# A product of token and row halves that needs no sum of weights moved from sixth to second place in each seven-product step

## The chip, the cores and the metric

The kernel runs on one core of a Trainium2 chip. The metric is the device time of one execution in microseconds (us); lower is better. The core's engines are TensorE (PE: matrix products; its loading of weights is listed as PEld), VectorE (DVE), ScalarE (ACT), GpSimd (POOL) and SyncE (SP), which here only starts transfers from HBM. Each engine works through its own queue in order, and engines wait for one another through semaphores.

## What is computed

One block of a decoder over 512 tokens with 1024 features, in float32. The change concerns the two feed-forward halves (`ffn1_*`, `ffn2_*`) alone; between them stand a gating mixer and a differential attention, which are not touched.

```python
def swiglu(h, w_gate, w_up, w_down):
    return (jax.nn.silu(h @ w_gate) * (h @ w_up)) @ w_down

x = x + 0.5 * swiglu(rms_norm(x, ffn1_norm), ffn1_w_gate, ffn1_w_up, ffn1_w_down)
...                                        # the mixer, another residual
x = x + 0.5 * swiglu(rms_norm(x, ffn2_norm), ffn2_w_gate, ffn2_w_up, ffn2_w_down)
```

`w_gate` and `w_up` are 1024 x 2816, `w_down` is 2816 x 1024.

## The kernel before

Data lies with features on the 128 partitions and tokens along the row, so x is 8 tiles of 128 x 512. To keep float32 accuracy each operand is split into a high and a low part: ScalarE casts the high part (line 139), VectorE subtracts it from the source (line 140), and a product is three matmuls, high x high, high x low and low x high. For weights the parts are `w_hi` and `w_lo`.

The 2816 inner features are taken 256 at a time, in 11 pieces numbered q. The first two of each half are computed plainly (`plain_quad`). The other nine go through `quad`, lines 304 to 363, and are called steps here: 18 in the kernel. A step regards its work as a product of 2 x 2 blocks: the tokens are cut into two halves of 256, the 1024 rows of the weights into two halves of 512, and the columns into gate and up. Instead of eight block products it makes seven, of sums of blocks. The block of weights b11 is gate of the first rows, b21 gate of the second rows, b12 and b22 the same for up. A11 and A12 are the first tokens with the first and the second rows, A22 the second tokens with the second rows; S0 to S3 are sums of such blocks, prepared once in each half by `half_sums`. A product, `product`, line 314, is named here after its operand. It splits its weights and makes 24 matmuls of 128 x 256 (all on line 324). In the order of the code a step is:

- A11 with b11 into bank a; ScalarE copies a as p1 (line 331)
- S1 with t3 = b12 + b22 into bank c; copied as p7
- S2 with t2 = t3 + b11, added into a; copied as u2
- A22 with t2 + b21, added into c; VectorE adds c and u2: the gate of the second tokens (line 346)
- S0 with b11 + b12, added into a; VectorE adds a into p7 (line 350)
- A12 with b21 into bank e; VectorE adds e and p1: the gate of the first tokens (line 352)
- the gate is multiplied by the norm's factors `r_bc` (line 357) and put through Silu on ScalarE (line 358)
- S3 with b22, added into a; VectorE multiplies a and p7 into the two halves of the gate (lines 360, 361), and the result is split as a_hi and a_lo

The sums of weights are made by VectorE (`total`, line 311). So bank a is written by A11, S2, S0 and S3 in turn, and read between them.

After four, four and three pieces the down projection adds their share, 8 products with matmuls of 128 x 512 (lines 125 to 127). This end of a group needs a_hi and a_lo of the last step from its nineteenth matmul on, its thirteenth in the third group.

Buffers set how far the splits run ahead. There are four pairs of w_hi and w_lo, used in turn, so the weights of a product go into the pair of four products before. There are six buffers for raw weights, used in turn too, four of them by a step (its loads are in the order b11, b12, b22, b21, by SyncE, line 307), and two for the sums.

The queue of each engine is laid out when the kernel is built: a scheduler goes by the order of the code and by its own estimates of how long operations take, and may put an instruction ahead of one that stands earlier in the code and would still have to wait. So the built order, and not the code alone, tells what stands behind what.

Of the kernel before, what the change touches and what calls it, by code (L numbers as in the profile page):

```python
# [17 lines left out]
ALU = mybir.AluOpType  # L18
# [28 lines left out]
HT = T // 2  # L47
# [11 lines left out]
def decoder_block(  # L59
# [25 lines left out]
    nc = tc.nc  # L85
# [10 lines left out]
    def bank(pool=acc):  # L96
        return pool.tile([P, T], F32, name="bank_" + pool.name, tag=pool.name)
# [3 lines left out]
    def any_bank():  # L101
        turn_of[0] ^= 1
        return bank(acc if turn_of[0] else att)

    def scratch():
        return tmp.tile([P, T], F32, name="scratch", tag="scratch")
# [31 lines left out]
    def split(hi, lo, src):  # L138
        latest["hi"] = nc.scalar.copy(hi, src)  # L139
        latest["lo"] = nc.vector.tensor_tensor(lo, src, hi, op=ALU.subtract)  # L140
# [104 lines left out]
    def ffn(pool, gu, dn, norm, xt, finish, load, prepare, again, plain):  # L245
# [4 lines left out]
        def parts():  # L250
            own = turns["w"] % 4 == 3
            turns["w"] += 1
            src = pool if own else wp
            return tuple(src.tile([P, 1024], F32R, name=f"w_{n}", tag=f"w_{n}") for n in ("hi", "lo"))

        def raw_tile():
            own = turns["raw"] % 6 > 1
            turns["raw"] += 1
            if own:
                return pool.tile([P, 1024], F32, name="w_raw", tag="w_raw", bufs=4)  # L260
            return wp.tile([P, 1024], F32, name="w_raw", tag="w_raw", bufs=RAWS)

        def activated(q):
            hi, lo = (pool.tile([P, 2, T], F32R, name=f"a_{n}{q}", tag=f"a_{n}{q % 4}") for n in ("hi", "lo"))
            a_hi[q], a_lo[q] = hi, lo
            return hi, lo

        def block(q, i):

            h = i // 2  # L270
            return gu[2 * q : 2 * q + 2, (i + h) % 2, :, h * T : (h + 1) * T].rearrange("f p c -> p f c")
# [30 lines left out]
            split(*activated(q), g)  # L302

        def quad(q):
            b11, b12, b22, b21 = (raw_tile() for _ in range(4))
            for i, t in enumerate((b11, b12, b22, b21)):
                nc.sync.dma_start(out=t.rearrange("p (f c) -> p f c", f=2), in_=block(q, i))

            def total(x, y):
                t = pool.tile([P, 1024], F32, name="w_sum", tag="w_sum", bufs=2)  # L310
                nc.vector.tensor_tensor(t, x, y, op=ALU.add)
                return t

            def product(ps, w, x, first=False):
                hi, lo = parts()
                split(hi, lo, w)
                of = operand(x)
                for f in range(2):
                    o = ps[:, f * HT : (f + 1) * HT]
                    for kt in range(HK):  # L320
                        s = slice((f * HK + kt) * P, (f * HK + kt + 1) * P)
                        x_hi, x_lo = of(kt)
                        for i, (l, r) in enumerate(((hi, x_hi), (hi, x_lo), (lo, x_hi))):
                            nc.tensor.matmul(  # L324
                                o, lhsT=l[:, s], rhs=r, start=first and f == kt == i == 0,
                                stop=kt == HK - 1 and i == 2, skip_group_check=True,
                            )

            def kept(ps):
                t = scratch()  # L330
                nc.scalar.copy(t, ps)
                return t

            two = dict(f=2)
            g = pool.tile([P, 2, T], F32, name="g", tag="g", bufs=2)
            a, c, e = bank(acc), bank(att), any_bank()
            product(a, b11, "A11", True)
            p1 = kept(a)
            t3 = total(b12, b22)
            product(c, t3, "S1", True)  # L340
            p7 = kept(c)
            t2 = total(t3, b11)
            product(a, t2, "S2")
            u2 = kept(a)
            product(c, total(t2, b21), "A22")
            nc.vector.tensor_tensor(
                g[:, :, HT:], c.rearrange("p (f t) -> p f t", **two), u2.rearrange("p (f t) -> p f t", **two), op=ALU.add
            )
            product(a, total(b11, b12), "S0")
            nc.vector.tensor_tensor(p7, a, p7, op=ALU.add)  # L350
            product(e, b21, "A12", True)
            nc.vector.tensor_tensor(
                g[:, :, :HT], e.rearrange("p (f t) -> p f t", **two), p1.rearrange("p (f t) -> p f t", **two), op=ALU.add
            )
            if q in prepare:
                prepare[q]()
            nc.vector.tensor_tensor(g, g, r_bc.unsqueeze(1).to_broadcast([P, 2, T]), op=ALU.mult)
            nc.scalar.activation(g, g, AF.Silu)
            product(a, b22, "S3")
            nc.vector.tensor_tensor(g[:, :, :HT], a.rearrange("p (f t) -> p f t", **two), g[:, :, :HT], op=ALU.mult)  # L360
            nc.vector.tensor_tensor(g[:, :, HT:], p7.rearrange("p (f t) -> p f t", **two), g[:, :, HT:], op=ALU.mult)
            split(*activated(q), g)

        y = []
        for f0 in range(0, NF, 8):
            n = min(8, NF - f0)
            for q in range(f0 // 2, (f0 + n) // 2):
                if q < plain:
                    plain_quad(q)
                else:  # L370
                    quad(q)
                if q == plain - 1:
                    for kt in range(HK):
                        add_sums(kt, xt[kt], xt[kt + HK])
            for j in range(KD):
# [21 lines left out]
                else:  # L397
                    for ts, ps in zip(cols, banks):
                        t = scratch()[:, ts]
# [646 lines left out]
```

## Time and profile before

| | us |
|---|---|
| median of 3 runs | 1154.8 |
| lowest, highest | 1154.61, 1155.35 |
| the profiled execution | 1154.97 |
| its span, first to last instruction | 1153.3 |
| TensorE busy | 1145.2 (99%) |
| VectorE busy | 845.9 (73%) |
| ScalarE busy | 590.7 (51%) |
| GpSimd busy | 28.6 (2%) |

The span is 1.7 us shorter than the execution, and TensorE is idle for some 8 us of it. Ends of matmuls are modelled and overlap, so in the rows below the distance from one matmul's start to the next says more than a matmul's length. The mean granted clock of TensorE is 1.000 over the span. A bracket at a row's end is the idle time of the engine just before and what ended it.

### The profile page before, as it was taken

Reading aid. Unit: us, or ns where it says so; the run is one execution under the profiler, and the core shown is the slowest. Engines: PE = TensorE matmul, PEld = TensorE weight load, DVE = VectorE, ACT = ScalarE, POOL = GpSimd, SP = SyncE. Lnnn points to the kernel's source line nnn. Section 1 sums busy time; section 2 is a strip of 40 time slices with the busy share of each in tenths; the row PEclk is TensorE's granted clock in tenths of the full one; section 3 lists DMA queues with packets and bytes.
Section 4 is the critical chain, followed back from the end, with each engine's and each line's share of the span. In section 5 each row is a group of like instructions: output and inputs, shape, how many; then the busy total and the mean of one; then the engine's idle time right before and its main releaser. Section 6 shows DMA issues by size and latency. Waiting matters only on the chain.

```text
span 1153.3 us, 16684 instructions
## 1 busy us (share of the span) xinstructions
PE 1145.2 (99%) x6568; PEld 996.8 (86%) x6568; DVE 845.9 (73%) x1374; ACT 590.7 (51%) x856; POOL 28.6 (2%) x57
## 2 busy tenths in 40 slices
PE   8999999999999999999999999999999999999998
PEld 7898899989987888888878887888899899988997
DVE  6985489768876767867878976655887369877874
ACT  6653356414544554667587966334545235523440
POOL 0000000000002000000000000000000000000000
PEclk9999999999999999999999999999999999999999
DMA  8144132623324323222212124334424223541222
GB/s 276 53 132 143 55 116 75 227 64 110 90 94 147 118 74 92 74 92 74 74 55 73 56 79 160 92 123 163 152 74 147 73 74 110 166 148 67 87 82 73
DMA packets 46861, 122.08 MB, mean 106 GB/s; under 512 B 4560, under 2 KB 5856, under 8 KB 46784
## 3 DMA queue, kind: packets, MB, share of 16 engines
q1 hardware_dynamic: 44208, 113.26, 30.7%
q0 software_dynamic: 2432, 7.75, 2.0%
q8 instruction: 51, 0.84, 0.3%
q14 instruction: 26, 0.21, 0.1%
q10 hardware_dynamic: 144, 0.01, 0.0%
HBM read 114.72 MB, written 6.29 MB: 105 GB/s over the span
## 4 chain that ended last, share of the span: by engine, by line
PE 95%; ACT 2%; DMA 1%; DVE 1%; issue 0%; SPq 0%; ACTq 0%; DVEq 0%
PE bank_acc L324 20%; PE bank_att L324 11%; PE bank_acc L127 11%; PE bank_acc L125 11%; PE bank_acc L126 11%; PE bank_att L127 5%; PE bank_att L126 5%; PE bank_att L125 5%; PE bank_acc L537 4%; PE bank_acc L539 4%; PE bank_acc L538 4%; DMA w_raw<-in_gu 1%; PE bank_att L667 1%; PE bank_att L668 1%; PE bank_att L695 1%
## 5 line engine op out<-in xcount | busy, mean ns | idle before, releaser
L139 ACT CAST w_hi<-w_raw 128x1024 fp32r<-128x1024 f32 (+2 forms) x192 | 191.8, 1004 | 281.2 <-PE bank_acc L126 91.8
L140 DVE TENSOR_TENSOR w_lo<-w_raw,w_hi 128x1024 fp32r<-128x1024 f32 (+2 forms) x192 | 224.0, 1170 | 78.2 <-ACT w_hi L139 73.3
L139 ACT CAST w_hi<-w_sum 128x1024 fp32r<-128x1024 f32 x72 | 75.5, 1050 | 138.7 <-PE bank_acc L324 62.0
L324 PE MATMUL bank_acc<-s_lo,w_hi 128*128 128x256 f32 x432 | 121.6, 281 | 0.0
L324 PE MATMUL bank_acc<-s_hi,w_hi 128*128 128x256 f32 x432 | 121.5, 281 | 0.0
L324 PE MATMUL bank_acc<-s_hi,w_lo 128*128 128x256 f32 x432 | 121.4, 281 | 0.0
L140 DVE TENSOR_TENSOR w_lo<-w_sum,w_hi 128x1024 fp32r<-128x1024 f32 x72 | 87.6, 1220 | 26.0 <-ACT w_hi L139 26.0
L125 PE MATMUL bank_acc<-xg_hi,w_hi 128*128 128x512 f32 x224 | 89.3, 399 | 1.3 <-ACT w_hi L139 1.3
L127 PE MATMUL bank_acc<-xg_hi,w_lo 128*128 128x512 f32 x224 | 89.2, 398 | 1.0 <-DVE w_lo L140 1.0
L537 PE MATMUL bank_acc<-w_hi,xg_hi 128*128 128x512 f32 x224 | 88.9, 397 | 0.0
L126 PE MATMUL bank_acc<-xg_lo,w_hi 128*128 128x512 f32 x224 | 88.8, 396 | 0.0
L538 PE MATMUL bank_acc<-w_lo,xg_hi 128*128 128x512 f32 x224 | 88.6, 395 | 0.0
L539 PE MATMUL bank_acc<-w_hi,xg_lo 128*128 128x512 f32 x224 | 88.5, 395 | 0.0
L324 PEld LDWEIGHTS bank_acc<-s_hi,w_hi 128*128 128x128 f32 x432 | 81.6, 189 | 0.0
L324 PEld LDWEIGHTS bank_acc<-s_hi,w_lo 128*128 128x128 f32 x432 | 81.7, 189 | 0.0
L324 PEld LDWEIGHTS bank_acc<-s_lo,w_hi 128*128 128x128 f32 x432 | 81.6, 189 | 0.0
L125 PE MATMUL bank_acc<-a_hi,w_hi 128*128 128x512 f32 (+1 forms) x182 | 71.1, 391 | 0.0
L126 PE MATMUL bank_acc<-a_lo,w_hi 128*128 128x512 f32 (+1 forms) x182 | 71.1, 391 | 0.0
L127 PE MATMUL bank_acc<-a_hi,w_lo 128*128 128x512 f32 (+1 forms) x182 | 71.1, 391 | 0.0
L126 PE MATMUL bank_att<-a_lo,w_hi 128*128 128x512 f32 (+1 forms) x176 | 68.7, 391 | 0.0
L125 PE MATMUL bank_att<-a_hi,w_hi 128*128 128x512 f32 (+1 forms) x176 | 68.7, 391 | 0.0
L127 PE MATMUL bank_att<-a_hi,w_lo 128*128 128x512 f32 (+1 forms) x176 | 68.7, 390 | 0.0
(270 smaller groups left out, 2847.2 us busy)
## 6 DMA issues: line engine op xcount, KB each, us to landing
w_raw<-in_gu SPq DMA_DIRECT2D x86, 512.0 KB, 3.8
w_raw<-in_dn SPq DMA_DIRECT2D x32, 512.0 KB, 3.8
w_raw<-in_w_qk SPq DMA_DIRECT2D x16, 512.0 KB, 3.6
w_raw<-in_dn SPq DMA_DIRECT2D x16, 384.0 KB, 3.1
w_raw<-in_w_v SPq DMA_DIRECT2D x8, 512.0 KB, 3.6
w_raw<-in_w_ga SPq DMA_DIRECT2D x8, 512.0 KB, 3.5
w_raw<-in_w_gb SPq DMA_DIRECT2D x8, 512.0 KB, 3.7
w_raw<-in_w_pb SPq DMA_DIRECT2D x8, 512.0 KB, 3.5
```

The source lines that it names most:

```text
L125: nc.tensor.matmul(ps, lhsT=lhi, rhs=rhi, start=first, stop=False)
L126: nc.tensor.matmul(ps, lhsT=lhi, rhs=rlo, start=False, stop=False)
L127: nc.tensor.matmul(ps, lhsT=llo, rhs=rhi, start=False, stop=last)
L139: latest["hi"] = nc.scalar.copy(hi, src)
L140: latest["lo"] = nc.vector.tensor_tensor(lo, src, hi, op=ALU.subtract)
L324: nc.tensor.matmul(o, lhsT=l[:, s], rhs=r, start=first and f == kt == i == 0, stop=kt == HK - 1 and i == 2, skip_group_check=True,)
L537: nc.tensor.matmul(banks[t], lhsT=xg_hi[k][:, ts], rhs=hi[:, s], start=k == 0, stop=False)
L538: nc.tensor.matmul(banks[t], lhsT=xg_hi[k][:, ts], rhs=lo[:, s], start=False, stop=False)
L539: nc.tensor.matmul(banks[t], lhsT=xg_lo[k][:, ts], rhs=hi[:, s], start=False, stop=k == KD - 1)
L667: nc.tensor.matmul(s[m], lhsT=qd[m][:, qs], rhs=kd[m][:, :w], start=True, stop=False)
L668: nc.tensor.matmul(s[m], lhsT=ql[m][:, qs], rhs=kd[m][:, :w], start=False, stop=True)
L695: nc.tensor.transpose(ps[:, j * P : (j + 1) * P], a[:, j * P : (j + 1) * P], ident)
```

## The change

The product A12 with its addition moves from behind S0 to behind A11, and the loads of a step go in the order b11, b21, b12, b22 instead of b11, b12, b22, b21. By this the addition of line 352 is line 340, that of line 346 is line 350, and that of line 350 is line 354; lines 357 to 361 keep their numbers. What is computed is the same.

```diff
@@ -302,8 +302,8 @@
         def quad(q):
-            b11, b12, b22, b21 = (raw_tile() for _ in range(4))
-            for i, t in enumerate((b11, b12, b22, b21)):
+            b11, b21, b12, b22 = (raw_tile() for _ in range(4))
+            for i, t in ((0, b11), (3, b21), (1, b12), (2, b22)):
                 nc.sync.dma_start(out=t.rearrange("p (f c) -> p f c", f=2), in_=block(q, i))
@@ -336,6 +336,10 @@
             product(a, b11, "A11", True)
             p1 = kept(a)
+            product(e, b21, "A12", True)
+            nc.vector.tensor_tensor(
+                g[:, :, :HT], e.rearrange("p (f t) -> p f t", **two), p1.rearrange("p (f t) -> p f t", **two), op=ALU.add
+            )
             t3 = total(b12, b22)
@@ -348,10 +352,6 @@
             product(a, total(b11, b12), "S0")
             nc.vector.tensor_tensor(p7, a, p7, op=ALU.add)
-            product(e, b21, "A12", True)
-            nc.vector.tensor_tensor(
-                g[:, :, :HT], e.rearrange("p (f t) -> p f t", **two), p1.rearrange("p (f t) -> p f t", **two), op=ALU.add
-            )
             if q in prepare:
```

Where it shows in the built order, first on TensorE in the first step of the second group (q = 4) of the first half: here bank_acc_1288 is a, bank_acc_1290 is e, and bank_acc_1521 is the a of the next step. Before, from the last two matmuls of S0 on:

```order
L324 MATMUL bank_acc_1288<-s_lo3_546,w_hi_1418 128x256
L324 MATMUL bank_acc_1288<-s_hi3_545,w_lo_1419 128x256
L324 MATMUL bank_acc_1290<-xg_hi4_104,w_hi_1447 128x256
L324 MATMUL bank_acc_1290<-xg_lo4_112,w_hi_1447 128x256
L324 MATMUL bank_acc_1290<-xg_hi4_104,w_lo_1448 128x256
```

All 24 matmuls of A12 into bank e stand there before S3 goes on in bank a. After, from the last matmul of S0 on:

```order
L324 MATMUL bank_acc_1288<-s_hi3_545,w_lo_1448 128x256
L324 MATMUL bank_acc_1521<-xg_hi0_100,w_hi_1524 128x256
L324 MATMUL bank_acc_1521<-xg_lo0_108,w_hi_1524 128x256
L324 MATMUL bank_acc_1521<-xg_hi0_100,w_lo_1525 128x256
L324 MATMUL bank_acc_1521<-xg_hi1_101,w_hi_1524 128x256
L324 MATMUL bank_acc_1521<-xg_lo1_109,w_hi_1524 128x256
L324 MATMUL bank_acc_1521<-xg_hi1_101,w_lo_1525 128x256
L324 MATMUL bank_acc_1521<-xg_hi2_102,w_hi_1524 128x256
L324 MATMUL bank_acc_1521<-xg_lo2_110,w_hi_1524 128x256
L324 MATMUL bank_acc_1521<-xg_hi2_102,w_lo_1525 128x256
L324 MATMUL bank_acc_1288<-s_hi0_512,w_hi_1478 128x256
```

Now nine matmuls of the next step's A11 stand between S0 and S3, and the other fifteen come behind S3. The number is 9 in ten of the 18 steps, and 11 and 15 in one each. In the last step of a group the down projection's matmuls stand there: 5 four times, 4 twice.

On VectorE at the same place, before:

```order
L140 TENSOR_TENSOR w_lo_1479<-w_raw_1281,w_hi_1478 128x1024
L346 TENSOR_TENSOR g_1287<-bank_att_1289,scratch_1383 128x2x256
L140 TENSOR_TENSOR w_lo_1525<-w_raw_1512,w_hi_1524 128x1024
L350 TENSOR_TENSOR scratch_1351<-bank_acc_1288,scratch_1351 128x512
L140 TENSOR_TENSOR w_lo_1557<-w_sum_1554,w_hi_1556 128x1024
L311 TENSOR_TENSOR w_sum_1618<-w_sum_1586,w_raw_1515 128x1024
L352 TENSOR_TENSOR g_1287<-bank_acc_1290,scratch_1319 128x2x256
```

and after:

```order
L140 TENSOR_TENSOR w_lo_1525<-w_raw_1512,w_hi_1524 128x1024
L350 TENSOR_TENSOR g_1287<-bank_att_1289,scratch_1412 128x2x256
L357 TENSOR_TENSOR g_1287<-g_1287,r_bc_116 128x1024
L140 TENSOR_TENSOR w_lo_1555<-w_raw_1513,w_hi_1554 128x1024
L354 TENSOR_TENSOR scratch_1380<-bank_acc_1288,scratch_1380 128x512
L361 TENSOR_TENSOR g_1287<-scratch_1380,g_1287 128x2x256
```

The multiplication by r_bc, which stood behind A12's addition, now stands with a split between the addition after A22 and the one after S0. In nine of the ten steps with 9 matmuls the order is this one; in the tenth, in the first step and in the last step of each half the split is ahead of line 357.

On TensorE at the end of the first group of the first half, in the first down product (bank_acc_1015), before:

```order
L127 MATMUL bank_acc_1015<-a_hi2_778,w_lo_1017 128x512
L125 MATMUL bank_acc_1015<-a_hi3_1011,w_hi_1016 128x512
L126 MATMUL bank_acc_1015<-a_lo3_1012,w_hi_1016 128x512
L127 MATMUL bank_acc_1015<-a_hi3_1011,w_lo_1017 128x512
L125 MATMUL bank_acc_1015<-a_hi3_1011,w_hi_1016 128x512
```

and after:

```order
L127 MATMUL bank_acc_1015<-a_hi2_778,w_lo_1017 128x512
L125 MATMUL bank_acc_1015<-a_hi3_1011,w_hi_1016 128x512
L125 MATMUL bank_att_1048<-a_hi0_366,w_hi_1049 128x512
L126 MATMUL bank_att_1048<-a_lo0_367,w_hi_1049 128x512
L126 MATMUL bank_acc_1015<-a_lo3_1012,w_hi_1016 128x512
```

Two matmuls of the second down product now stand ahead of the first that reads a_lo of the last step; five of the first down product's matmuls have moved ahead of S3.

## Rows read from the trace of the kernel before

**Rows 1.** The page: span, busy time by engine, the chain that ended last.

```profile
span 1153.3 us, 16684 instructions
PE 1145.2 (99%) x6568; PEld 996.8 (86%) x6568; DVE 845.9 (73%) x1374; ACT 590.7 (51%) x856; POOL 28.6 (2%) x57
PE 95%; ACT 2%; DMA 1%; DVE 1%; issue 0%; SPq 0%; ACTq 0%; DVEq 0%
```

**Rows 2.** Waits of TensorE: who waited for whom, total us, times, longest.

```profile
PE bank_acc L125 <- ACT w_hi L139: 1.3, 1, 1.3
```

**Rows 3.** Chain in order of time, one step's A22: start, us, what.

```profile
270.65 2.84 PE bank_att L324 x24
```

**Rows 4.** Stretch of steps: PE, PEld, DVE, ACT, POOL busy, clock, DMA, GB/s.

```profile
262.00:282.00 20.00, 20.00 (x171) 20.00 (x170) 16.31 (x17) 8.77 (x11) 0.00 (x0) 1.00 0.31 106
```

**Rows 5.** Timeline of TensorE, step q = 8: S0's first, last, A12's first, S3's first.

```profile
273.32 0.28 PE L324 MATMUL bank_acc<-s_hi,w_hi 128*128 128x256 f32 x1
...
276.05 0.27 PE L324 MATMUL bank_acc<-s_hi,w_lo 128*128 128x256 f32 x1
276.16 0.28 PE L324 MATMUL bank_acc<-xg_hi,w_hi 128*128 128x256 f32 x1
...
279.03 0.28 PE L324 MATMUL bank_acc<-s_hi,w_hi 128*128 128x256 f32 x1
```

**Rows 6.** Timeline of VectorE in the same step.

```profile
273.59 0.69 DVE L346 TENSOR_TENSOR g<-bank_att,scratch 128x512 f32<-128x512 f32 x1 [0.68 <-PE bank_att L324]
274.49 1.23 DVE L140 TENSOR_TENSOR w_lo<-w_raw,w_hi 128x1024 fp32r<-128x1024 f32 x1 [0.20 <-ACT w_hi L139]
276.36 0.69 DVE L350 TENSOR_TENSOR scratch<-bank_acc,scratch 128x512 f32<-128x512 f32 x1 [0.65 <-PE bank_acc L324]
```

**Rows 7.** Timeline of VectorE, step q = 4: two instructions that wait for nothing.

```profile
157.31 1.22 DVE L357 TENSOR_TENSOR g<-g,r_bc 128x1024 f32<-128x1024 f32 x1
158.45 1.22 DVE L311 TENSOR_TENSOR w_sum<-w_raw 128x1024 f32<-128x1024 f32 x1
```

**Rows 8.** Timeline of TensorE, end of the first half's third group.

```profile
326.08 0.49 PE L125 MATMUL bank_att<-a_hi,w_hi 128*128 128x512 f32 x1
326.41 0.39 PE L126 MATMUL bank_acc<-a_lo,w_hi 128*128 128x512 f32 x1
326.64 0.40 PE L127 MATMUL bank_acc<-a_hi,w_lo 128*128 128x512 f32 x1
...
327.34 0.50 PE L126 MATMUL bank_att<-a_lo,w_hi 128*128 128x512 f32 x1
327.68 0.39 PE L127 MATMUL bank_att<-a_hi,w_lo 128*128 128x512 f32 x1
```

**Rows 9.** Timeline of ScalarE at the same place: the cast that 326.08 waits for.

```profile
324.98 1.05 ACT L139 CAST a_hi<-g 128x1024 fp32r<-128x1024 f32 x1 [1.41 <-DVE g L361]
```

**Rows 10.** Timeline of TensorE and VectorE, first step: S0's last, S3's first two.

```profile
67.49 0.28 PE L324 MATMUL bank_acc<-s_hi,w_lo 128*128 128x256 f32 x1
...
69.63 0.68 DVE L350 TENSOR_TENSOR scratch<-bank_acc,scratch 128x512 f32<-128x512 f32 x1
70.46 0.36 PE L324 MATMUL bank_acc<-s_hi,w_hi 128*128 128x256 f32 x1
70.65 0.28 PE L324 MATMUL bank_acc<-s_lo,w_hi 128*128 128x256 f32 x1
```

**Rows 11.** Timeline of ScalarE in the step of rows 5.

```profile
273.41 1.05 ACT L139 CAST w_hi<-w_raw 128x1024 fp32r<-128x1024 f32 x1 [1.26 <-PE bank_att L324]
```

**Rows 12.** Timeline of VectorE, step q = 5: a small instruction of the constants.

```profile
170.80 0.28 DVE L426 TENSOR_TENSOR scratch<-scratch 128x128 f32<-128x128 f32 x1
```

**Rows 13.** TensorE at the kernel's start: a stretch (columns of rows 4), timeline.

```profile
5.00:9.00 4.00, 3.60 (x9) 2.93 (x10) 2.63 (x5) 2.59 (x7) 0.00 (x0) 1.00 0.94 294
5.40 0.79 PE L125 MATMUL bank_acc<-xg_hi,w_hi 128*128 128x512 f32 x1 [1.33 <-ACT w_hi L139]
5.99 0.63 PE L125 MATMUL bank_att<-xg_hi,w_hi 128*128 128x512 f32 x1
25.53 0.50 PE L127 MATMUL bank_acc<-xg_hi,w_lo 128*128 128x512 f32 x1 [1.04 <-DVE w_lo L140]
```

## The prediction

> **What bounds the kernel now.** First the page's busy times and its chain of work: TensorE is busy 1145.2 of 1153.3 us and holds 95% of the chain that ended last [rows 1]. Then the list of who waited for whom on TensorE: six entries, the longest 1.3 us [rows 2], all of them at the kernel's start or in the mixing part; in the steps (the seven products of `quad`) it waits for nothing it lists, so nothing there is left to win on TensorE. The chain in order of time gives the price of a product: 24 matmuls in 2.84 us, 0.118 us from one start to the next [rows 3]. VectorE is the next bound: 16.31 of 20 us are busy in a stretch of steps [rows 4]. So an edit to the steps can cost by making TensorE wait, and can gain almost nothing.
>
> **What is removed, added, moved.** No instruction is added: 18 steps of seven products, the same splits, sums and gating operations. Moving A12 and its addition (line 352, then 340) puts A12's 2.84 us in another place and is worth nothing by itself. On SyncE's queue b21 goes from fourth to second of a step's loads. This lies far ahead of use: the third load still takes the buffer of b11, free after the sum b11+b12 of the step before, and S1, the first to need it, still starts four products after S0 of the step before (S0, A12, S3, A11 stand between now; S0, S3, A11, A12 later). GpSimd's queue is untouched, and ScalarE's copy p1 has a product more of slack. I take 0 for these, with 0.5 us as the most they could cost.
>
> What does change is the cover behind S0. S0 and S3 accumulate in the same bank, and between them VectorE must read it (line 350; 354 in the changed code: "the p7 addition"). Now A12 lies there: S0's last matmul starts at 276.05, the addition at 276.36, and S3 at 279.03, 2.67 us after the addition [rows 5, 6]. Afterwards S3 would follow S0 directly, so the built order puts matmuls of the next product there: 9 of the next A11 in ten steps, 11 and 15 in one step each, and where a group of steps ends, 5 (four times) or 4 (twice) of the down projection.
>
> **The step with 9 matmuls.** Let 0 be the start of S0, 273.32 [rows 5]; by its place S3 would start at 2.84 + 9 x 0.118 = 3.90. VectorE first does the addition after A22 (line 346; 350 afterwards), which now starts at 273.59, so at 0.27, and takes 0.69 [rows 6]. The built order then has, in nine of these ten steps, the multiplication by r_bc (line 357), one split (line 140), and the p7 addition. Line 357 needs the addition's result: 0.98. Where nothing is waited for, VectorE starts the next instruction 1.14 us after one of 1024 elements, a little under its length [rows 7]: split at 2.12, p7 addition at 3.26. S0's result is there by 2.84 + 0.20 = 3.04 (S0's slot ends at 276.16, the addition starts at 276.36 [rows 5, 6]), so it needn't wait: 3.26 + 0.69 = 3.95, and with 0.05 to the waiting engine (a_hi ends at 326.03, its matmul begins at 326.08 [rows 8, 9]) 4.00. S3 is 0.10 late.
>
> A matmul that is held has a second price. At 326.08 and 327.34 two matmuls of the down projection waited for operands that came just when they were due, and each took 0.33 to 0.34 us to the next start, where 0.23 is usual [rows 8]: 0.10 each. The nearest row of a 256-column matmul is in the first step: S3 at 70.46, held by the p7 addition that ran from 69.63 to 70.31, then 0.19 instead of 0.12 [rows 10], 0.07. I take 0.08, so 0.18 per step and 1.6 us for nine. If VectorE is 0.2 earlier, all of it is covered, 0; were one more split ahead of the p7 addition, it would be 1.3 per step (both are rivals, below).
>
> The Trainium skill ("TensorE: Matmul & The Clock Gate", section "Single matmul latency") gives an isolated matmul about 166 ns beyond its columns. If each of some two dozen held matmuls paid this instead of the 0.07 to 0.10 of the rows, the sum would be about 1.7 us higher; the rows decide here.
>
> **The other steps.** In the tenth step with 9 the order is split, line 357, p7 addition. That split waits for ScalarE's cast, which starts when A22's weights are released (273.41 [rows 11]), so it starts as now at 274.49, 1.17 after the origin [rows 6]; line 357 at 2.31, p7 at 3.45, done and seen at 4.19: 0.29 late, 0.37 with the restart. The step with 11, the first, has that order too: S3's place is 4.14, 0.05 late; but VectorE is behind there (its p7 addition now runs at 69.63, 2.14 after the start of S0's last matmul at 67.49 [rows 10], where 0.31 is usual). A12 gives it 2.84 us of matmuls for one split of 1.14, so the lag should be small: 0.3, between 0 and 1.5. The step with 15 has constants of the mixing part in VectorE's queue: nine small instructions (0.28 for one of the longest [rows 12]) between the addition and p7, about 1.1 us beyond 4.00, against a place of 4.61; 0.6, between 0 and 1.5.
>
> Where a group ends, the 5 matmuls of 512 columns are 5 x 0.233, so S3's place is 4.00, just when it is released: 0.1 each, 0.4 for four. With 4 it is 3.77, behind a split of 768 columns (an estimate of 0.86 from the 1.14), p7 seen at about 3.77: 0.2 for two. Behind S3 the first down product needs the last step's a_hi and a_lo five matmuls earlier than now, and the built order has two matmuls of the next product ahead of a_lo. From S3's end to a_lo VectorE and ScalarE have line 360, two casts, a split and a_lo itself: about 3.75 us, against 16 x 0.233 = 3.73. So one held matmul of 0.12 at four boundaries, 0.5, between 0 and 1; the two boundaries with 4 have such holds already [rows 8].
>
> **Sum.** 1.6 + 0.4 + 0.3 + 0.6 + 0.4 + 0.2 + 0.5 = 4.0 us, less the 0.07 that the first step pays already: 3.9. The profiled execution took 1154.97 us around its span of 1153.3 [rows 1]; with 3.9 it would take 1158.9. The median of the runs before is 0.2 lower, so I predict **1158.7 us**. About 0.2%, or 2.3 us, is what a measurement of this kernel can tell from no change.
>
> **Rivals.** (a) *Covered.* If VectorE comes to the p7 addition 0.2 us earlier than worked out, the 9 matmuls hide it entirely; a wait that is met in time costs nothing now (S0 to A12, 276.05 to 276.16 [rows 5]). What is left is some 0.5 to 1.5 us of group ends and the first step: 1155.9, not slower by the bound above. For it: the fillers come out within 0.1 us of my ready times in most steps. Against: the two matmuls of rows 8 stood just as close to their operands, and both paid 0.10.
> (b) *VectorE is behind.* If the addition after A22 isn't prompt, p7 slips with it. Now it starts 0.38 to 0.41 after A22's last matmul in 15 of 18 steps, and 0.9 to 1.7 later than that in three (the first, and the two with the constants). It decides whether one more instruction of 1.14 gets in front. In twelve of the steps that is 12 x 1.14 = 13.7 on top, about 1172; in four, 1163. Against: before that addition VectorE will have less to do than now, since lines 352, 357 and 361 of the step before are done earlier.
> (c) *Faster.* Only waits that exist can vanish: four held matmuls in the third groups and one in the first step, 0.5 us: 1154.3, which is no measurable change either. Faster by more would need a wait that the trace doesn't show.
> (d) *Clock.* At the kernel's start, after TensorE had stood still for 1.33 us, it ran nine matmuls of 512 columns in 4 us, 0.43 apart instead of 0.23: the pace of the 1.2 GHz level, though the granted clock reads 1.00 there [rows 13]. If each of 18 holds did that, 3.6 us at half pace lose 1.7 us apiece: 1185. Against: after the hold of 1.04 us before 25.53 the matmul took 0.50 and not the 0.63 of the start [rows 13], and the holds forecast here are 0.1 to 0.4. The Trainium skill names such a case ("TensorE: Matmul & The Clock Gate", section "A second HAM failure mode: psum-queue depth-cycling": frequent short idling between groups of matmuls makes the clock swing); the rows don't bear it out for holds as short as these.
> That the change doesn't do what it says is out: the built order has A12 second in all 18 steps.
>
> **How the numbers follow.** My forecast (1156.5 to 1161.5) 0.60; (a) 0.25; (b) 0.08; (c) 0.05, of which 0.02 for a wait that the trace hides and that would make it faster by over the bound; (d) 0.02. A tenth of the forecast's chance lies under 1157.1, so slower by over 0.2% has 0.54 + 0.10 = 0.64; within 0.2% has 0.06 + 0.25 + 0.03 = 0.34; faster 0.02. The range takes in the unknown costs, most of (a) and the small end of (b): 1155.4 to 1163.5.
>
> **What would show it.** In the profile after: TensorE waits on line 324 for VectorE's p7 addition (line 354), 10 to 18 times, 0.1 to 0.3 us each, 2 to 4 us in all, where now it lists none; products still 2.84; S3's first matmul about 0.19 long to the next; the p7 addition 3.2 to 3.3 after S0's start in a plain step; a held matmul at a_lo in the first two groups of each half. If p7 starts at 3.05 instead, (a) is right; if at 4.4, with one more instruction of 1.14 before it, (b). If TensorE waits in the steps for a split or a load instead, my reading of the queues is wrong.

## The result, and the profile after

The changed kernel takes 1161.7 us in the median of 4 runs (1160.62 to 1162.66), the kernel before 1154.7 beside it; the ratio is 1.0058, with an interval of 1.0045 to 1.0070. It is slower, by 7.0 us in the medians. The profiled execution is one of the shorter runs, 1160.82 us, and is 5.85 us longer than that of before; its span grew from 1153.3 to 1159.1 us. The two longer runs are 2 us above it. A further series of five runs (below) lay between 1160.44 and 1161.14, so what the two had more is not explained here. Two runs of the experiments below, one of 1388.7 us at a granted clock of 0.753 and one of 3285.8 us, are slow ones and are left out of every median and ratio.

On the page TensorE is still busy for 99% of the span, but the chain that ended last now goes through VectorE for 4% of it, where it was 1% [rows 1]:

```profile
span 1159.1 us, 16666 instructions
PE 1149.0 (99%) x6568; PEld 996.9 (86%) x6568; DVE 845.5 (73%) x1374; ACT 587.5 (51%) x855; POOL 28.7 (2%) x57
PE 90%; DVE 4%; ACT 2%; DMA 2%; issue 1%; SPq 0%; DVEq 0%; ACTq 0%
```

TensorE's waits (who waited for whom, total us, times, longest) have a new first entry, where [rows 2] had none in the steps:

```profile
PE bank_acc L324 <- DVE scratch L354: 2.7, 5, 1.1
```

This is S3 waiting for the p7 addition (line 354). The list shows five of these waits. In the timeline all 18 are to be seen, since the distance of two starts also shows a wait that is too short to be listed. A plain step, the q = 8 of [rows 5] and [rows 6], on VectorE and then on TensorE, from S0's last matmul through the nine of the next A11 to S3:

```profile
278.95 0.69 DVE L350 TENSOR_TENSOR g<-bank_att,scratch 128x512 f32<-128x512 f32 x1 [0.67 <-PE bank_att L324]
279.68 1.23 DVE L357 TENSOR_TENSOR g<-g,r_bc 128x1024 f32<-128x1024 f32 x1
280.82 1.22 DVE L140 TENSOR_TENSOR w_lo<-w_raw,w_hi 128x1024 fp32r<-128x1024 f32 x1
281.96 0.68 DVE L354 TENSOR_TENSOR scratch<-bank_acc,scratch 128x512 f32<-128x512 f32 x1
```

```profile
281.43 0.28 PE L324 MATMUL bank_acc<-s_hi,w_lo 128*128 128x256 f32 x1
281.55 0.28 PE L324 MATMUL bank_acc<-xg_hi,w_hi 128*128 128x256 f32 x1
...
282.49 0.28 PE L324 MATMUL bank_acc<-xg_hi,w_lo 128*128 128x256 f32 x1
282.69 0.39 PE L324 MATMUL bank_acc<-s_hi,w_hi 128*128 128x256 f32 x1
282.92 0.28 PE L324 MATMUL bank_acc<-s_lo,w_hi 128*128 128x256 f32 x1
```

The p7 addition ends at 282.64 and S3 begins at 282.69. By its place S3 would have begun 0.118 after 282.49, at 282.61: it is 0.08 late. From its own start to the next is 0.23 instead of 0.12; this extra 0.11 is called the restart here. The two parts, the lateness and the restart, can be read off for each of the 18 steps:

| steps | how many | forecast, us in all | lateness, restart of one | measured, us in all |
|---|---|---|---|---|
| 9 matmuls, as above | 7 | 1.3 of the 1.6 | 0.08 to 0.11, 0.10 | 1.4 |
| 9 matmuls: first half q = 4; second half's first step | 2 | 0.3 of the 1.6 | 0.45 and 1.22, 0.10 | 1.9 |
| 9 matmuls, split ahead of line 357 (q = 6) | 1 | 0.4 | 0.55, 0.10 | 0.65 |
| 11 matmuls, first step of the first half | 1 | 0.3 | 0.94, 0.11 | 1.05 |
| 15 matmuls, constants (q = 5) | 1 | 0.6 | 0.36, 0.10 | 0.5 |
| end of a group, 5 matmuls | 4 | 0.4 | 0.02, 0.10 | 0.5 |
| end of a group, 4 matmuls | 2 | 0.2 | 0.02 to 0.03, 0.10 | 0.25 |
| a_lo at group ends | 4 | 0.5 | none | 0 |
| sum | | 4.0 | | 6.2 |

So the 6.2 us in the steps are the whole loss of the profiled execution. From the first matmul of line 324 to the mixing part the kernel took 305.4 us (302.0 before), from there to the second half 492.0 (492.0), and from the second half's first such matmul to TensorE's last 304.6 (301.8): the mixing part lost nothing.

The large entries come from VectorE. In the second half's first step, with the two loads that SyncE issues together first, then VectorE, then TensorE:

```profile
855.02 1.59 SPq L307 DMA_DIRECT2D w_raw<-in_gu  x2
```

```profile
861.51 1.23 DVE L311 TENSOR_TENSOR w_sum<-w_raw 128x1024 f32<-128x1024 f32 x1 [1.29 <-DMA w_raw<-in_gu]
862.65 1.22 DVE L140 TENSOR_TENSOR w_lo<-w_raw,w_hi 128x1024 fp32r<-128x1024 f32 x1
863.79 1.22 DVE L311 TENSOR_TENSOR w_sum<-w_sum,w_raw 128x1024 f32<-128x1024 f32 x1
864.93 1.22 DVE L140 TENSOR_TENSOR w_lo<-w_raw,w_hi 128x1024 fp32r<-128x1024 f32 x1
866.06 0.69 DVE L350 TENSOR_TENSOR g<-bank_att,scratch 128x512 f32<-128x512 f32 x1
866.78 1.22 DVE L357 TENSOR_TENSOR g<-g,r_bc 128x1024 f32<-128x1024 f32 x1
867.93 1.22 DVE L140 TENSOR_TENSOR w_lo<-w_raw,w_hi 128x1024 fp32r<-128x1024 f32 x1
869.06 0.68 DVE L354 TENSOR_TENSOR scratch<-bank_acc,scratch 128x512 f32<-128x512 f32 x1
```

```profile
864.56 0.28 PE L324 MATMUL bank_att<-xg_hi,w_lo 128*128 128x256 f32 x1
...
868.46 0.28 PE L324 MATMUL bank_acc<-xg_hi,w_lo 128*128 128x256 f32 x1
869.80 0.38 PE L324 MATMUL bank_acc<-s_hi,w_hi 128*128 128x256 f32 x1 [1.06 <-DVE scratch L354]
870.02 0.28 PE L324 MATMUL bank_acc<-s_lo,w_hi 128*128 128x256 f32 x1
```

A22's last matmul starts at 864.56, so the addition after it (line 350) was due at about 864.95. It begins at 866.06, with no idle time before it: VectorE has been working without a gap since 861.51. There it had waited 1.29 us for a load, in the sum t3 = b12 + b22 that the next step needs. The addition came 1.1 late by this, p7 with it, and S3 1.22 late.

In q = 6 the same sum waited 0.40 us for its load. In the first half's first step it hardly waited. The first three rows are of this step, the last is of q = 6:

```profile
63.98 1.23 DVE L140 TENSOR_TENSOR w_lo<-w_sum,w_hi 128x1024 fp32r<-128x1024 f32 x1 [1.17 <-ACT w_hi L139]
65.12 1.22 DVE L140 TENSOR_TENSOR w_lo<-w_raw,w_hi 128x1024 fp32r<-128x1024 f32 x1
66.44 1.23 DVE L311 TENSOR_TENSOR w_sum<-w_raw 128x1024 f32<-128x1024 f32 x1
...
193.29 1.23 DVE L311 TENSOR_TENSOR w_sum<-w_raw 128x1024 f32<-128x1024 f32 x1 [0.40 <-DMA w_raw<-in_gu]
```

From 65.12 to 66.44 is 1.32, where 1.14 is usual: 0.18 of waiting. Here VectorE had stood for 1.17 us behind a cast of ScalarE, and the sum with its own length of 1.14 came in front of line 350 all the same, which began at 68.72, 1.2 late.

### The profile page after: what moved, and what is told of

Read it like the earlier page. It is cut to its first block, busy times and chain, and to the rows that moved or that the text cites. A ratio compares the mean times of both kernels' runs of the same rounds, so it can differ in the third digit from the quotient of the medians.

```text
span 1159.1 us, 16666 instructions
## 1 busy us (share of the span) xinstructions
PE 1149.0 (99%) x6568; PEld 996.9 (86%) x6568; DVE 845.5 (73%) x1374; ACT 587.5 (51%) x855; POOL 28.7 (2%) x57
## 4 chain that ended last, share of the span: by engine, by line
PE 90%; DVE 4%; ACT 2%; DMA 2%; issue 1%; SPq 0%; DVEq 0%; ACTq 0%
PE bank_acc L324 17%; PE bank_acc L127 11%; PE bank_acc L125 11%; PE bank_acc L126 11%; PE bank_att L324 10%; PE bank_att L126 5%; PE bank_att L127 5%; PE bank_att L125 5%; PE bank_acc L537 4%; PE bank_acc L539 4%; PE bank_acc L538 4%; DMA w_raw<-in_gu 2%; DVE w_lo L140 1%; PE bank_att L667 1%; PE bank_att L668 1%
```

## Experiments

The theory at the start was the prediction's: all of the loss is S3 held behind the p7 addition, once by a plain margin of 0.1 and a restart of 0.1, and in a few steps by more. Open was what made it more, and whether the moved product or the moved loads cost anything in other ways. The kernel before was run beside each of the three series: 1154.95, 1154.56 and 1154.52 us in the median. In every profiled execution the granted clock is 1.000.

### The product moved, the loads in the old order

```diff
-            b11, b21, b12, b22 = (raw_tile() for _ in range(4))
-            for i, t in ((0, b11), (3, b21), (1, b12), (2, b22)):
+            b11, b12, b22, b21 = (raw_tile() for _ in range(4))
+            for i, t in enumerate((b11, b12, b22, b21)):
```

> A12 second as in the changed kernel, but the four loads of a step in the order of before (b11, b12, b22, b21). Theory (the time is lost where S3 waits for VectorE's reading of bank a behind S0): the waits on line 354 stay, 18 of them with 0.1 late and 0.1 restart in plain steps, and the time is that of the changed kernel within 1.5 us, 1160 to 1163; only the lag of VectorE in the first steps may differ. Rival (the order of the loads makes it: b12 and b22 land later and VectorE waits for them ahead of its other work): the time falls back to 1155 to 1157 and the waits in the first steps of both halves vanish. If b21 loaded fourth comes too late for A12, TensorE waits for a split of A12 instead, which the profile would show on line 324.

Measured: 1158.1 us, ratio 1.0026 (1.0017 to 1.0036), between the two. All 18 holds are still there, the plain ones as above, but the lateness in both first steps is 0.11, in q = 4 0.08 and in q = 6 0.05; only q = 5 keeps 0.48. The sum over the steps is 3.5 us. VectorE in the second half's first step:

```profile
858.31 1.22 DVE L311 TENSOR_TENSOR w_sum<-w_raw 128x1024 f32<-128x1024 f32 x1
...
863.11 0.69 DVE L350 TENSOR_TENSOR g<-bank_att,scratch 128x512 f32<-128x512 f32 x1 [0.18 <-PE bank_att L324]
```

The sum t3 stands at the same place of the queue, but finds its data there, and the addition of line 350 waits for TensorE and not the other way round. So the new order of loads is worth about 3 us of the loss (2.7 to 3.0 between the traces, 2.6 to 3.0 between the medians), which I had taken for 0, with 0.5 at most.

### The loads moved, the products in the old order

```diff
-            b11, b12, b22, b21 = (raw_tile() for _ in range(4))
-            for i, t in enumerate((b11, b12, b22, b21)):
+            b11, b21, b12, b22 = (raw_tile() for _ in range(4))
+            for i, t in ((0, b11), (3, b21), (1, b12), (2, b22)):
```

> The order of products as before (A12 sixth), only the loads in the new order (b11, b21, b12, b22). Theory: 1154 to 1156, no measurable change, no wait of TensorE in the steps. Rival (loads): 1157 or more, with VectorE waiting longer for w_raw before the sums of line 311 and TensorE for splits.

Measured: 1154.7 us, ratio 1.0000 (0.9991 to 1.0009), and no hold in any step. VectorE's waits for these loads did grow, from 11.3 us in 10 times to this:

```profile
DVE w_sum L311 <- DMA w_raw<-in_gu: 15.2, 12, 3.8
```

With A12 behind S0 they cost nothing. The loads alone are harmless; it takes the missing cover to make VectorE's lag count.

### Another product as the cover

In this kernel the order is A11, A12, S2, S1, S0, A22, S3, so that A22 with its 24 matmuls stands between S0 and S3.

```diff
             t3 = total(b12, b22)
-            product(c, t3, "S1", True)
-            p7 = kept(c)
             t2 = total(t3, b11)
             product(a, t2, "S2")
             u2 = kept(a)
+            product(c, t3, "S1", True)
+            p7 = kept(c)
+            product(a, total(b11, b12), "S0")
+            nc.vector.tensor_tensor(p7, a, p7, op=ALU.add)
             product(c, total(t2, b21), "A22")
...
-            product(a, total(b11, b12), "S0")
-            nc.vector.tensor_tensor(p7, a, p7, op=ALU.add)
```

> A12 stays second, but S2 goes ahead of S1 and A22 behind S0, so that a whole product stands between any two uses of banks a and c again (A11, A12, S2, S1, S0, A22, S3). Theory: the waits of S3 vanish, products follow one another at 2.84, and the time is 1154.5 to 1157, the rest being a few held matmuls at group ends and in two steps where the scheduler still puts matmuls of the next A11 in between. Rival (A12 in second place itself crowds VectorE, whatever stands behind S0): 1159 or more, with TensorE waiting for splits in the steps.

Measured: 1157.9 us, ratio 1.0027 (1.0018 to 1.0036), above the 1154.5 to 1157 of the theory. The holds of S3 are gone in 17 of 18 steps. Of the 2.6 us that are left, 0.2 are the eighteenth; the rest is another wait, around the steps with the constants of the mixing part:

```profile
PE bank_acc L324 <- DVE w_lo L140: 1.0, 2, 0.8
PE bank_att L324 <- DVE w_lo L140: 0.5, 1, 0.5
```

TensorE waits there for a split of weights; the second half, which has no such constants, takes 302.0 us, 0.2 more than before. The experiment shows that a product behind S0 removes the holds, but its time alone doesn't show it, since this order has a cost of its own.

### The p7 addition ahead of the multiplication by r_bc

```diff
-            nc.vector.tensor_tensor(p7, a, p7, op=ALU.add)
+            read = nc.vector.tensor_tensor(p7, a, p7, op=ALU.add)
...
-            nc.vector.tensor_tensor(g, g, r_bc.unsqueeze(1).to_broadcast([P, 2, T]), op=ALU.mult)
+            in_turn(nc.vector.tensor_tensor(g, g, r_bc.unsqueeze(1).to_broadcast([P, 2, T]), op=ALU.mult), read)
```

> The changed kernel, with the multiplication of line 357 held behind the p7 addition (line 354) on VectorE, so that one instruction of 1.14 less stands ahead of the addition; the scheduler then fills 8 matmuls instead of 9 and 4 instead of 5. Theory: p7 starts about 0.2 after S0's slot, is done at 3.78 where S3's place is 2.84 + 8 x 0.118 = 3.78, so lateness goes to 0.0 to 0.05 but the restart of 0.10 stays in all 18 steps: 1156.5 to 1159, some 2 to 4 us under the changed kernel. Rival (the cost is a fixed one of switching banks between S0 and S3, whatever VectorE does): 1161 as the changed kernel.

Measured: 1159.1 us, ratio 1.0035 (1.0022 to 1.0047), at the upper end of the theory's 1156.5 to 1159. In a plain step VectorE is now ready first and waits for S0:

```profile
281.02 0.69 DVE L354 TENSOR_TENSOR scratch<-bank_acc,scratch 128x512 f32<-128x512 f32 x1 [0.68 <-PE bank_acc L324]
```

S3 starts at 281.76, just at its place: the built order has 8 matmuls there now, and no lateness. Yet the restart stays, 0.10 to 0.11 in all 18 steps. An operand that arrives exactly in time still costs 0.10. The lateness in the first half's first step (1.06) and in q = 5 (0.65) stays as well, the one in the second half's first step is gone, and the sum is 3.7 us.

### S3 into a bank of its own

```diff
-            product(a, b22, "S3")
-            nc.vector.tensor_tensor(g[:, :, :HT], a.rearrange("p (f t) -> p f t", **two), g[:, :, :HT], op=ALU.mult)
+            product(e, b22, "S3", True)
+            nc.vector.tensor_tensor(g[:, :, :HT], e.rearrange("p (f t) -> p f t", **two), g[:, :, :HT], op=ALU.mult)
```

> The changed kernel, but S3 goes into bank e (free since A12's addition) and not into a; the sum of S3 with A11, S2 and S0 is left out of the gate. The new order of products and loads stays, and in the built order S3's 24 matmuls follow S0's directly, with no matmul of another product between. Theory (everything the change costs is TensorE held at S3 because bank a must be read first): no hold at S3 in any of the 18 steps, VectorE's lag in the first steps stays visible but costs nothing, 1154.9 us (1154.3 to 1155.6). Rival (with A12 second, the loads or splits hold TensorE by themselves as well): 1157 to 1159, with waits on weights or loads in the first steps.

Measured: 1154.8 us, ratio 1.0001 (0.9992 to 1.0010), in a kernel whose gate leaves out the sum of S3 with the other three products. The second half's first step, S0's last matmul and S3's first on TensorE, then VectorE:

```profile
864.25 0.28 PE L324 MATMUL bank_acc<-s_hi,w_lo 128*128 128x256 f32 x1
864.37 0.28 PE L324 MATMUL bank_att<-s_hi,w_hi 128*128 128x256 f32 x1
864.49 0.28 PE L324 MATMUL bank_att<-s_lo,w_hi 128*128 128x256 f32 x1
```

```profile
859.02 1.23 DVE L311 TENSOR_TENSOR w_sum<-w_raw 128x1024 f32<-128x1024 f32 x1 [1.95 <-DMA w_raw<-in_gu]
...
866.57 0.68 DVE L354 TENSOR_TENSOR scratch<-bank_acc,scratch 128x512 f32<-128x512 f32 x1
```

VectorE is as late as in the changed kernel, the p7 addition 2.2 us behind S0, and TensorE doesn't notice: starts 0.12 apart from S0 into S3. The whole loss hangs on bank a being shared. Neither the place of A12 nor the loads cost TensorE anything by another path: no step of this trace has a hold, and the time is that of before within 1 us.

### The sum of the next step behind the p7 addition

Loads and products as changed; t3 is held in VectorE's queue until the p7 addition of the step before stands ahead of it.

```diff
+        before = [None]
...
-            def total(x, y):
+            def total(x, y, behind=None):
...
-                nc.vector.tensor_tensor(t, x, y, op=ALU.add)
+                in_turn(nc.vector.tensor_tensor(t, x, y, op=ALU.add), behind)
...
-            t3 = total(b12, b22)
+            t3 = total(b12, b22, before[0])
...
-            nc.vector.tensor_tensor(p7, a, p7, op=ALU.add)
+            before[0] = nc.vector.tensor_tensor(p7, a, p7, op=ALU.add)
```

> The changed kernel, with one order added on VectorE: the sum t3 of the next step (b12 + b22) stands behind the addition of S0 into p7 of the step before, so that its wait for a load can't delay that addition. Loads and products stay as changed. Theory (the part of the loss beyond the kernel with the old order of loads, some 3 us, is this one chain: load, t3, addition after A22, p7, S3): S3 is 0.1 late in the first steps of both halves and at most 0.1 in q = 6, where it was 0.94, 1.22 and 0.55; sum of lateness and restarts 3.3 to 4.0 us, time 1158.1 (1157.4 to 1158.9). Rival (the new order of loads costs in another way, as by later weights): 1160 to 1162, S3 still about 1 us late in the first steps.

Measured: 1157.6 us, ratio 1.0024 (1.0015 to 1.0034), 3.2 us less than the changed kernel in the same series. VectorE in the second half's first step:

```profile
863.33 0.69 DVE L350 TENSOR_TENSOR g<-bank_att,scratch 128x512 f32<-128x512 f32 x1 [0.67 <-PE bank_att L324]
...
866.33 0.68 DVE L354 TENSOR_TENSOR scratch<-bank_acc,scratch 128x512 f32<-128x512 f32 x1
866.93 1.22 DVE L311 TENSOR_TENSOR w_sum<-w_raw 128x1024 f32<-128x1024 f32 x1
```

The addition of line 350 waits for TensorE again, t3 comes behind line 354, and S3 is 0.11 late as in a plain step; so in the first half's first step, and 0.03 in q = 6. The sum is 3.2 us. The built order also has 12 and 13 matmuls as cover in q = 6 and q = 5, which is some of the gain there. With the loads unchanged, it is t3 ahead of the addition after A22, and so of p7 and S3, that makes the additional loss in the first steps. How much of this is the wait for the load and how much the sum's own length differs from step to step, as said above.

### Both cuts

Old order of loads and the p7 addition ahead of line 357: the first edit and the `in_turn` edit above together.

> A12 second, loads in the old order, and line 357 held behind the addition of S0 into p7. Theory (the two cuts are of different parts and add): restarts of 0.10 in all 18 steps, 1.8 us, the plain steps 0.0 late, the step with the constants some 0.5 late; sum 2.1 to 2.8 us, time 1157.0 (1156.3 to 1157.8). Rival (both take away the same thing): about 1158, as with the old loads alone.

Measured: 1157.6 us, ratio 1.0024 (1.0015 to 1.0034): inside the range of the theory, but 0.6 above its figure. 17 steps pay the restart alone, as expected. The step with the constants is worse than expected, 1.18 late, since seven of its small instructions now stand between lines 350 and 354:

```profile
177.29 0.39 PE L324 MATMUL bank_acc<-s_hi,w_hi 128*128 128x256 f32 x1 [1.03 <-DVE scratch L354]
```

Sum 3.2 us. The plain lateness is gone, but one step gave most of that back. By its time alone the kernel can't be told from the rival's (about 1158, as with the old loads): both are 3 us above the kernel before, and only the trace shows that the two cuts act on different parts.

### The changed kernel again

> The changed kernel once more, for a second trace. Theory (the lags of the first steps belong to the built order and the loads): S3 again 0.9 to 1.2 late in the first steps of both halves, 1160.5 to 1162.7 us. If the 0.45 of q = 4 belongs to the order too, it stands there again; if it is a chance of one execution, S3 is 0.1 late there.

Measured: 1160.7 us (1160.44 to 1161.14), ratio 1.0051 (1.0038 to 1.0064). The second trace has the same steps: 0.93 and 1.55 in the first steps, 0.47 in q = 6, 0.38 in q = 5, 0.45 in q = 4; sum 6.5 us. So the q = 4 of the first half belongs to the built order and not to one execution. Line 350 there, in the first trace and the second:

```profile
153.35 0.69 DVE L350 TENSOR_TENSOR g<-bank_att,scratch 128x512 f32<-128x512 f32 x1 [1.04 <-PE bank_att L324]
```

```profile
153.14 0.69 DVE L350 TENSOR_TENSOR g<-bank_att,scratch 128x512 f32<-128x512 f32 x1 [1.04 <-PE bank_att L324]
```

VectorE was idle before it, and A22's last matmul had started 0.75 us earlier, where 0.38 is usual. What it waited for in that third of a microsecond the trace doesn't tell; it stays open. In the next kernel (S3 behind A11) the same lag stands in the q = 4 of the second half and not of the first.

### S3 behind the whole A11 of the next step

Line 359 to the end of `quad` becomes a function that the next step calls when its A11 is written; at the end of a group it is called ahead of the down projection.

```diff
+        late = []
...
             p1 = kept(a)
+            last_product()
             product(e, b21, "A12", True)
...
-            product(a, b22, "S3")
+            def rest():
+                product(a, b22, "S3")
...
+            late.append(rest)
+
+        def last_product():
+            if late:
+                late.pop()()
```

> The changed kernel (A12 second, loads in the new order), but inside a group S3 is written behind the whole A11 of the next step, so that 24 matmuls stand between S0 and S3 where 9, 11 or 15 stood; at the six ends of a group nothing changes. Theory (the loss is only too short a cover behind S0): no hold at S3 in the twelve steps inside a group, also not in the first steps, where VectorE's lag stays; 0.12 to 0.13 at each of the six group ends, 0.7 us; time 1155.4 (1154.7 to 1156.3). Rival (S3 moved on makes the gate, its split or the buffers of b22 late somewhere else): 1157 or more, with waits of TensorE for weights or for a load.

Measured: 1155.6 us in the median, ratio 1.0009 (1.0000 to 1.0018). The second half's first step, VectorE (line 351 is the addition after A22, line 355 that into p7) and TensorE from S0's last matmul over A11 (its 24 matmuls lie between 863.82 and 866.54) to S3:

```profile
862.61 0.68 DVE L351 TENSOR_TENSOR g<-bank_att,scratch 128x512 f32<-128x512 f32 x1
...
865.61 0.68 DVE L355 TENSOR_TENSOR scratch<-bank_acc,scratch 128x512 f32<-128x512 f32 x1
```

```profile
863.70 0.28 PE L324 MATMUL bank_acc<-s_hi,w_lo 128*128 128x256 f32 x1
...
866.54 0.27 PE L324 MATMUL bank_acc<-xg_hi,w_lo 128*128 128x256 f32 x1
866.65 0.28 PE L324 MATMUL bank_acc<-s_hi,w_hi 128*128 128x256 f32 x1
866.77 0.28 PE L324 MATMUL bank_acc<-s_lo,w_hi 128*128 128x256 f32 x1
```

The p7 addition is 1.8 us behind S0, later than in the changed kernel's 1.5, and S3 starts in its place all the same. In the twelve steps inside a group nothing is held; at the six group ends 0.12 to 0.13 each, 0.73 in all, as worked out. This gives back all but about 1 us of the loss with A12 still second. It is not faster than the kernel before. It also shows that the 0.10 of a held S3 is no price of going back to bank a: in the twelve steps TensorE goes back to it too, and the start after S3's first is 0.11 to 0.12 later as usual.

### All of them side by side

| kernel | held in the steps, us | median less that of before beside it, us |
|---|---|---|
| changed, again | 6.5 | 6.2 |
| changed, p7 addition first | 3.7 | 4.1 |
| changed, old loads | 3.5 | 3.2 |
| changed, t3 behind p7 | 3.2 | 3.0 |
| changed, old loads and p7 first | 3.2 | 3.0 |
| A22 as the cover | 2.6 | 2.9 |
| changed, S3 behind A11 | 0.7 | 1.1 |
| changed, S3 in its own bank | 0 | 0.3 |
| before, new loads | 0 | -0.2 |

What TensorE is held in the steps is what each kernel is slower by, within 0.4 us. The interval of each of these times is about 1 us to either side, so nothing larger than that is left to be explained, and the order of kernels that lie closer together rests on the traces. Only the 7.0 us of the first series are more than the 6.2 to 6.5 held.

## Why the prediction held, point by point

**The time: inside the range, above the forecast.** The median of 1161.7 lies just above the forecast's own band (1156.5 to 1161.5) and inside the range that was kept for unknown costs. The steps lost 6.2 us where 4.0 was worked out, and most of what was missing lies in one term, the loads.

**Mechanism: right.** The cover behind S0 was what counted. S3 in its own bank (0.3 us slower than before) and S3 behind 24 matmuls (1.1) show it from two sides.

**The plain step: right, to 0.02.** S3 released at 4.00 after S0's start and 0.10 late was the forecast; seven steps have 0.08 to 0.11. VectorE's instructions follow one another at 1.14 as in [rows 7]. The steps at group ends came out at 0.12 each, where 0.10 was set.

**The restart: a little too small.** I took 0.08, between the 0.07 of [rows 10] and the 0.10 of [rows 8]; it is 0.10 to 0.11 in 18 of 18 steps, also where S3 is not late at all. The row of the other shape of matmul was the better one. S3 of [rows 10] was not held, though the prediction takes it so: 25 matmuls of 0.118 after 67.49 its place is 70.44, and it starts at 70.46, 0.15 after the addition's end, where a held S3 starts 0.05 to 0.06 after it. So its 0.07 was the price of a small margin and not of a hold. The Trainium skill's figure ("TensorE: Matmul & The Clock Gate", section "Single matmul latency": about 166 ns beyond the columns for a bf16 matmul by itself) is not reached: a matmul held in the midst of a stream pays 0.10 here.

**The loads: the step that failed.** "I take 0 for these, with 0.5 us as the most they could cost" was argued from TensorE's side: S1 starts four products later. But the load is first used by VectorE, in the sum t3, and that sum stands in VectorE's queue ahead of the addition after A22 of the step before. In the old order t3 needs the second and third load of a step, in the new one the third and fourth, which SyncE issues together (855.02). Where loads are tight, VectorE stands at t3 (1.29 us in the second half's first step, 0.40 in q = 6), and the addition that TensorE waits for stands behind it; in the first half's first step it is the sum's own length that is in the way. This made both first steps and q = 6 cost 3.0 us together, where they had 0.9; the old loads, or t3 moved, take it away. The Trainium skill ("Perfetto Trace Analysis", section "Tensor Engine Instruction (MATMUL, LD_WEIGHTS)") says that VectorE's queue is strictly first in, first out. The 1.1 us by which line 350 is late with no idle time before it agree.

**Rival (b) came in part.** "Before that addition VectorE will have less to do than now" is true of the count of instructions and missed the wait among them. The rival had the right place; it came in two steps with about one instruction's length, and in q = 6 with half of one, and not in four or twelve.

**q = 4: not foreseen and not explained.** 0.35 us of the sum. With the old loads and with t3 moved S3 is 0.08 late there, so these 0.35 are in the 3 us that both kernels gain; but the kernels with S3 in its own bank and with p7 first have the new loads and no such lag, so it isn't shown to come from the loads.

**The step with the constants: about right,** 0.46 for 0.6.

**a_lo at the group ends: wrong.** I worked out 3.75 us from S3's end to a_lo with two casts and a split between. In the first group of the first half the first of the two casts ran beside line 360 and not behind it. First ScalarE, then line 360 and a_lo on VectorE with TensorE:

```profile
95.28 1.05 ACT L139 CAST w_hi<-w_raw 128x1024 fp32r<-128x1024 f32 x1 [2.83 <-issue]
```

```profile
95.35 0.69 DVE L360 TENSOR_TENSOR g<-bank_acc,g 128x512 f32<-128x512 f32 x1 [1.26 <-PE bank_acc L324]
97.51 1.22 DVE L140 TENSOR_TENSOR a_lo<-g,a_hi 128x1024 fp32r<-128x1024 f32 x1
98.64 0.40 PE L126 MATMUL bank_att<-a_lo,w_hi 128*128 128x512 f32 x1
98.88 0.39 PE L126 MATMUL bank_acc<-a_lo,w_hi 128*128 128x512 f32 x1
```

a_lo ends at 98.73, 3.58 after S3's slot ended at 95.15, and the first matmul that reads it (of the first down product, bank_acc) is due at 98.88. The 0.5 us forecast here hid a part of what the loads added: the sum was 4.0 for 6.2 measured, with one term 0.5 too high and the others 2.7 too low.

**Covered, and the clock: no.** The nine matmuls were 0.1 us short in the plain steps, and rival (a) needed all of it. In the profiled executions the granted clock is 1.000 with 18 holds as it was with none in the steps. The case of a swinging clock that the Trainium skill describes ("TensorE: Matmul & The Clock Gate", section "A second HAM failure mode: psum-queue depth-cycling") doesn't show with holds of up to 1.55 us in these executions.

## What to carry to other kernels

Two products that accumulate in one bank with a read between them need other work between them. It has to last as long as the reading engine's queue can be late, and not only as long as the read itself takes: here the nine matmuls that a scheduler put there were 0.1 us short in the steady steps and 0.5 to 1.5 us short where a sum stood ahead of the read. When a load is moved, look for its first user in the queue of every engine, and for what stands behind that user. And give cover with a margin: an operand that came exactly in time still cost the 0.10 of a restart here.

## What the runs showed of the hardware

A matmul of 128 x 256 whose operand is released at the moment it is due takes 0.22 to 0.23 us to the next start instead of 0.118, whether it was 0.00 or 1.5 us late. I had not expected the price to be so even: 0.10 to 0.11 in every held step of the traces. How much margin makes it vanish can be narrowed down by the distance from the end of the p7 addition to the start of S3. At 0.05 to 0.06 S3 is held and pays 0.10 to 0.11. At 0.15 it paid 0.07 ([rows 10]), at 0.14 only 0.01, in the first step of the kernel with only the loads moved, where the addition ends at 69.29 and S3's second matmul starts at 69.56:

```profile
69.43 0.30 PE L324 MATMUL bank_acc<-s_hi,w_hi 128*128 128x256 f32 x1
```

From 0.32 on (in that kernel; 0.36 with S3 behind A11) it was free in every step.
